# A decoder step with tanh gates, decays queued after attention, sample products among later projections and state updates queued after each FFN block

## The chip, the cores and the metric

The kernel runs on one core of one Trainium2 chip. The metric is the time of one execution in microseconds, as the device counts it; lower is better.

## The reference

One layer of a hybrid decoder, for a prompt of 256 tokens and for 8 sequences that each add one token (264 columns in all). All is fp32. Cut to what matters here:

```python
D_MODEL = 2048; SEQ = 256; DEC_BATCH = 8; WINDOW = 128
SSD_HEADS = 32; SSD_HEAD_DIM = 64; D_STATE = 128; D_FF = 5632

def ssd_mixer(z, xbc, dt_raw, ...):
    xbc, conv_new = causal_dwconv(xbc, conv_past, conv_w, conv_b)
    ...
    y, h_last = ssd_scan(xs, dt, a, bm, cm, h0, chunk)     # chunks of 128
    y = y + xs * d_skip
    y = y.reshape(b, t, D_SSD) * jax.nn.silu(z)
    y = rms_norm(y, norm_g)
    return y, conv_new, h_last

def conv_ffn(x, past, g_ffn, w_up, conv_w, conv_b, w_down):
    u, new_past = causal_dwconv(rms_norm(x, g_ffn) @ w_up, past, conv_w, conv_b)
    gate, val = jnp.split(u, 2, axis=-1)
    return (jax.nn.silu(gate) * val) @ w_down, new_past

def _layer(x, ...):
    proj = rms_norm(x, g_mix) @ w_in            # q | k | v | z | x,B,C | dt
    attn = swa_banded(...)                      # or swa_step for the 8 samples
    ssd, new_conv, new_h = ssd_mixer(...)
    x = x + concatenate([attn, ssd]) @ w_out
    x = x + cross_attend(x, mem_k, mem_v, ...)  # 256 memory tokens
    f, new_ffn = conv_ffn(x, ...)
    return x + f, (new_k, new_v, new_conv, new_h, new_ffn)
```

Inside `ssd_scan`, the decay between two tokens of a chunk is `exp(la_l - la_s)` for l >= s. The new states of the 8 samples, `h * exp(dt a) + x dt B`, are an output of 32 heads x 64 x 128 numbers for each sample.

## The kernel before, in words

Features lie on the 128 partitions, and the 264 tokens are the columns. A matrix product in fp32 is made of three products of split numbers, high x high, high x low and low x high (`mm3`, lines 102 to 104). The weights stream: `weights` (L69) starts the load of a unit of 128 x 2048 numbers (1 MB, `wraw`, two buffers) on SyncE's queue; ScalarE casts each half of it to `whi` (L87), and VectorE subtracts to get `wlo` (L88). `whi` and `wlo` have four buffers each, so the casts can be at most four halves ahead of TensorE. One half feeds 24 matmuls of 264 columns. The second operand, the activations, is split in the same way (`split`, L92).

The stages follow each other in the span: the input projection with q, k and dt (to about 100 us), windowed attention for the prompt (`attn_prompt`) and the samples, x, B and C with their convolution (`conv_group`), the scan of the prompt by groups (`ssd_prompt`, with the decays `e`), the gate (`z_pair`, eight pairs of 128 features, from about 345 us), the output projection `w_out` (its attention half first, eight units, `AT`; then the half of the scan, `Y`), cross attention, and the FFN from about 675 us to the end. In the FFN, 44 blocks each take two `w_up` units, are evacuated (`u`, L1074), convolved (`c`, L1089 on ScalarE, L1091 on VectorE), gated with Silu (L1093) and split (`hh`, `hl`); after each group of eight blocks come units of `w_dn`.

The work for the 8 samples goes along: `ssd_sample(g)` loads old states on GpSimd's DMA queue (L691) and makes the products C*h on VectorE (L692, L693); `gate_sample` combines them to `ysam`, gates and splits it into the last columns of `Y`; `new_state(k, q)` loads old states `hn` on SyncE's queue (512 KB for two calls, three buffers), scales them on ScalarE (L1046), adds x dt B on VectorE (L1047) and stores them from GpSimd's queue (L1050). `memory_norm` loads the memory tokens `mraw` into a pool that opens after the mixer's pool is closed, so these loads come after what the mixer's pool still does, `gate_sample` among it. `accy` sums the squares of the gated y for its norm; `ry` is the reciprocal root of it.

The order of instructions on each engine is made by the scheduler from a simulated timeline; an engine then runs its instructions in that order, and waits at the head of its queue. `tc.high_priority()` lets weight casts go first, and `tc.issue_after(x)` puts what it encloses behind instruction x in the order. Queues that matter: ScalarE, VectorE, GpSimd (also issuing DMAs), SyncE (issuing DMAs).

Of the kernel before, what the change touches and what calls it, by code (L numbers as in the profile page):

```python
# [7 lines left out]
F32 = mybir.dt.float32  # L8
F32R = mybir.dt.float32r
AF = mybir.ActivationFunctionType  # L10
ALU = mybir.AluOpType
# [3 lines left out]
D = 2048  # L15
# [32 lines left out]
def hybrid_decoder_step_kernel(ctx: ExitStack, tc: tile.TileContext, I, O):  # L48
# [166 lines left out]
    def sumsq(acc, x, first, w=T):  # L215
        if first:
            S.activation(out=acc, in_=x, func=AF.Square)
        else:
            sq = small.tile([128, T], F32, tag="sq", name="sq")
            S.activation(out=sq[:, :w], in_=x, func=AF.Square)  # L220
            P.tensor_tensor(out=acc, in0=acc, in1=sq[:, :w], op=ALU.add)
# [23 lines left out]
    gssd = pc("g_ssd", 0, KB)  # L245
# [185 lines left out]
    def attn_prompt(j, rq, nrq):  # L431
        pp = j // 4
        for c in range(2):
# [34 lines left out]
            S.copy(out=attn[:, j, c * 128:c * 128 + 128], in_=o[:, 0:128])  # L468

    pq = psum("s")  # L470
# [145 lines left out]
    def ssd_prompt(g):  # L616
        hs = slice(8 * g, 8 * g + 8)
        hp = mp.tile([128, 512], F32, tag="hp", name="hp", bufs=1)
        for c in range(2):
# [6 lines left out]
            for hh in range(2):  # L626
# [4 lines left out]
                for j in range(4):  # L631
                    S.activation(out=e[:, j, :], in_=e[:, j, :], func=AF.Relu, scale=-1.0, bias=la[:, c * 32 + h0 + j:c * 32 + h0 + j + 1])
                S.activation(out=e, in_=e, func=AF.Exp, scale=-1.0)
# [74 lines left out]
    def z_pair(i):  # L708
# [9 lines left out]
        for m in range(2):  # L718
            k = 2 * i + m
            z = zs[m]  # L720
            S.activation(out=z, in_=z, func=AF.Silu)
            y = xs[k // 4][:, k % 4, :TP]
            V.tensor_tensor(out=y, in0=z, in1=y, op=ALU.mult)
            sumsq(accy[:, :TP], y, k == 0, TP)
            split(Y[k // 8][0][:, k % 8, :TP], Y[k // 8][1][:, k % 8, :TP], y, gssd[:, k:k + 1])

    def gate_sample():
# [7 lines left out]
        S.activation(out=zsam, in_=zsam, func=AF.Silu)  # L735
        V.tensor_tensor(out=ysam, in0=ysam, in1=zsam, op=ALU.mult)
        V.tensor_tensor(out=t, in0=ysam, in1=ysam, op=ALU.mult)
# [20 lines left out]
    ssd_sample(1)  # L758
# [3 lines left out]
    ssd_sample(2)  # L762
    ssd_prompt(3)
    for i in range(2, 8):
        z_pair(i)
        if i == 2:
            ssd_sample(3)
        if i in (3, 5, 7):
            res_load()
# [23 lines left out]
    for i in range(8):  # L793
# [5 lines left out]
        if i == 0:  # L799
            gate_sample()  # L800
    ry = total(accy, D, "ry")
# [258 lines left out]

    groups = [list(range(8 * g, min(8 * g + 8, FB))) for g in range(6)]
    w_up, w_dn = I["w_up"], I["w_dn"]

    def up(g):
        H = (T3(apool, 8, F32R, "A", f"hh{g}", 4), T3(apool, 8, F32R, "A", f"hl{g}", 4))
        n = len(groups[g])
        for ii, i in enumerate(groups[g]):
            us = []

            def ev(m, pm, i=i):  # L1070
# [3 lines left out]
                V.tensor_tensor(out=u[:, 2:], in0=pm, in1=r2, op=ALU.mult)  # L1074
# [5 lines left out]
            if 4 <= i < 36:  # L1080
                new_state(i // 2 - 2, i % 2)
            cs = []
            for m in range(2):
# [5 lines left out]
                S.activation(out=c, in_=u[:, 0:TP], func=AF.Identity, scale=w[0], bias=pc("fb", bi))  # L1089
                for t in (1, 2):  # L1090
                    V.scalar_tensor_tensor(out=c, in0=u[:, t:t + TP], scalar=w[t], in1=c, op0=ALU.mult, op1=ALU.add)  # L1091
                cs.append(c)
            S.activation(out=cs[0], in_=cs[0], func=AF.Silu)  # L1093
# [187 lines left out]
```

## Time and profile before

| | us |
|---|---|
| three runs | 1460.23, 1462.5, 1462.5 (median 1462.5) |
| profiled execution | 1458.88 |
| its span, first to last instruction | 1457.1 |
| granted TensorE clock, mean | 0.991 |
| busy: TensorE / VectorE / ScalarE / GpSimd | 1422.7 / 1062.6 / 790.7 / 176.3 |
| DMA | 304.65 MB, mean 209 GB/s |

A row of a timeline has a start, a length, the engine, the line, the operation, out<-in and the count; the bracket at its end tells how long the engine was idle before it and what ended that. A row of groups has the busy time, the mean of one in ns and the idle time before. A row of stretches has start and end, and for each engine the busy time and the number of instructions.

### The profile page before, as it was taken

How to read it: one execution, taken by the hardware profiler on the slowest of the kernel's cores; microseconds unless marked ns; L12 is line 12 of the kernel's file. 1: busy time of each engine (PE TensorE's matmuls, PEld its weight loads, DVE VectorE, ACT ScalarE, POOL GpSimd, SP SyncE). 2: the span in 40 equal slices, each digit the busy share in tenths (PEclk: the TensorE clock that was granted, in tenths of full speed). 3: DMA queues.
4: the chain of work that ended last, by engine and by line, in shares of the span. 5: the costliest groups of instructions: out<-in, count | busy, mean ns of one | idle time of the engine just before them, and what ended most of it. 6: DMA issues, size and time to landing. Idle time of an engine off the chain costs nothing.

```text
span 1457.1 us, 28707 instructions
## 1 busy us (share of the span) xinstructions
PE 1422.7 (98%) x11481; PEld 1394.7 (96%) x11481; DVE 1062.6 (73%) x2033; ACT 790.7 (54%) x1308; POOL 176.3 (12%) x345
## 2 busy tenths in 40 slices
PE   9999999998999999989899999999999999999999
PEld 8998899998899999979899999999999999999999
DVE  6839869998867667779898666667566756665664
ACT  6647745568646456558786453445345434543442
POOL 0000001123214113116112010001000000000000
PEclk9999999999999999999999999999999999999999
DMA  7754346766675555966898555555555455555554
GB/s 257 281 171 145 118 167 212 251 235 225 232 266 184 190 179 204 344 249 251 320 336 291 193 177 176 184 190 175 177 186 188 174 179 188 183 174 180 191 190 148
DMA packets 59366, 304.65 MB, mean 209 GB/s; under 512 B 8864, under 2 KB 13920, under 8 KB 29664
## 3 DMA queue, kind: packets, MB, share of 16 engines
q1 hardware_dynamic: 53728, 283.94, 55.7%
q0 software_dynamic: 5504, 18.88, 3.6%
q8 instruction: 90, 1.47, 0.4%
q14 instruction: 44, 0.36, 0.1%
HBM read 287.06 MB, written 16.28 MB: 208 GB/s over the span
## 4 chain that ended last, share of the span: by engine, by line
PE 80%; DMA 7%; DVE 6%; ACT 4%; issue 2%; POOL 1%; SPq 0%; ACTq 0%; DVEq 0%; POOLq 0%
PE mm L102 17%; PE mm L103 17%; PE mm L104 17%; PE t L102 8%; PE t L104 8%; PE t L103 8%; DVE wlo L88 2%; DMA wraw<-in_w_up_dram 2%; ACT whi L87 1%; DMA wraw<-in_w_out_dram 1%; DMA hn<-in_h_dram 1%; DVE hn L1047 1%; DMA wraw<-in_w_in_dram 1%; PE s L437 1%; POOL qq L871 1%
## 5 line engine op out<-in xcount | busy, mean ns | idle before, releaser
L87 ACT CAST whi<-wraw 128x1024 fp32r<-128x1024 f32 x448 | 464.9, 1049 | 531.2 <-PE mm L103 297.2
L88 DVE TENSOR_TENSOR wlo<-wraw,whi 128x1024 fp32r<-128x1024 f32 x448 | 552.2, 1237 | 260.8 <-ACT whi L87 257.2
L104 PE MATMUL t<-x2h,wlo 128*128 128x264 f32 x704 | 198.5, 285 | 4.2 <-DVE wlo L88 4.2
L102 PE MATMUL t<-x2h,whi 128*128 128x264 f32 x704 | 200.2, 285 | 1.5 <-ACT whi L87 1.5
L102 PE MATMUL mm<-x2h,whi 128*128 128x264 f32 x704 | 199.4, 284 | 0.6 <-DVE res L1015 0.6
L103 PE MATMUL t<-x2l,whi 128*128 128x264 f32 x704 | 199.7, 284 | 0.0
L104 PE MATMUL mm<-x2h,wlo 128*128 128x264 f32 x704 | 197.4, 284 | 2.3 <-DVE wlo L88 2.3
L103 PE MATMUL mm<-x2l,whi 128*128 128x264 f32 x704 | 199.2, 284 | 0.0
L103 PE MATMUL mm<-hl,whi 128*128 128x264 f32 x704 | 198.8, 283 | 0.0
L104 PE MATMUL mm<-hh,wlo 128*128 128x264 f32 x704 | 198.6, 283 | 0.0
L102 PE MATMUL mm<-hh,whi 128*128 128x264 f32 x704 | 196.9, 284 | 0.0
L102 PE MATMUL mm<-xh,whi 128*128 128x264 f32 x608 | 177.2, 293 | 0.0
L103 PE MATMUL mm<-xl,whi 128*128 128x264 f32 x608 | 176.2, 291 | 0.0
L104 PE MATMUL mm<-xh,wlo 128*128 128x264 f32 x608 | 175.4, 293 | 0.5 <-DVE wlo L88 0.5
L104 PEld LDWEIGHTS t<-x2h,wlo 128*128 128x128 f32 x704 | 132.0, 189 | 5.1 <-DVE wlo L88 5.1
L102 PEld LDWEIGHTS t<-x2h,whi 128*128 128x128 f32 x704 | 133.2, 189 | 1.7 <-ACT whi L87 1.7
L104 PEld LDWEIGHTS mm<-x2h,wlo 128*128 128x128 f32 x704 | 131.1, 188 | 3.2 <-DVE wlo L88 3.2
L102 PEld LDWEIGHTS mm<-x2h,whi 128*128 128x128 f32 x704 | 132.4, 188 | 1.0 <-issue 0.8
L103 PEld LDWEIGHTS t<-x2l,whi 128*128 128x128 f32 x704 | 133.2, 189 | 0.0
L103 PEld LDWEIGHTS mm<-x2l,whi 128*128 128x128 f32 x704 | 132.5, 188 | 0.0
L103 PEld LDWEIGHTS mm<-hl,whi 128*128 128x128 f32 x704 | 132.4, 188 | 0.0
L104 PEld LDWEIGHTS mm<-hh,wlo 128*128 128x128 f32 x704 | 132.2, 188 | 0.0
(418 smaller groups left out, 3075.1 us busy)
## 6 DMA issues: line engine op xcount, KB each, us to landing
wraw<-in_w_up_dram SPq DMA_DIRECT2D x88, 1024.0 KB, 4.9
wraw<-in_w_in_dram SPq DMA_DIRECT2D x51, 1024.0 KB, 5.1
wraw<-in_w_dn_dram SPq DMA_DIRECT2D x44, 1024.0 KB, 4.9
wraw<-in_w_out_dram SPq DMA_DIRECT2D x24, 1024.0 KB, 4.9
h<-in_h_dram POOLq DMA_DIRECT2D x32, 256.0 KB, 4.4
hn<-in_h_dram SPq DMA_DIRECT2D x16, 512.0 KB, 7.5
out_state_s_dram<-hn POOLq DMA_DIRECT2D x16, 512.0 KB, 6.5
pb<-dram_p SPq DMA_DIRECT2D x4, 1028.0 KB, 10.3
```

The lines of the kernel that those rows point to most:

```text
L87: S.copy(out=hi, in_=x)
L88: V.tensor_tensor(out=lo, in0=x, in1=hi.bitcast(F32), op=ALU.subtract)
L102: PE.matmul(out, wh, xh, start=start, stop=False)
L103: PE.matmul(out, wh, xl, start=False, stop=False)
L104: PE.matmul(out, wl, xh, start=False, stop=stop)
L437: PE.matmul(s3, qT[:, j, c * 128:c * 128 + 128], kbd[:, pp, :, 0:nk], start=True, stop=True)
L871: P.tensor_copy(out=qq[:, :, m], in_=sqs[m][:, TP:T])
L1047: V.scalar_tensor_tensor(out=h[:, b, :], in0=bbs[g][:, b, :], scalar=xds[:, k, b:b + 1], in1=h[:, b, :], op0=ALU.mult, op1=ALU.add)
```

## The change

It has four parts.

1. The gate Silu(z) * y becomes (1 + tanh(z/2)) * z * y, one tanh on ScalarE into a new tile `th`, and one more VectorE instruction; the factor 2 is taken up by halving the norm's gain `gssd` and by dividing the sum of squares by 4D. The same holds for the samples in `gate_sample`. The 15 adds of `accy` go from GpSimd to VectorE.
2. The ScalarE part of the decays `e` (four Relu, one Exp each) is issued only after the last copy of the prompt's attention output.
3. `ssd_sample(1)`, `(2)` and `(3)` move to later places among the z pairs and into `w_out`, `gate_sample` from the first to the fifth of the eight attention units of `w_out`.
4. `new_state` of a FFN block moves behind that block's own evacuation and its own ScalarE convolution.

```diff
-    def sumsq(acc, x, first, w=T):
+    def sumsq(acc, x, first, w=T, on=P):
...
-            P.tensor_tensor(out=acc, in0=acc, in1=sq[:, :w], op=ALU.add)
+            on.tensor_tensor(out=acc, in0=acc, in1=sq[:, :w], op=ALU.add)
...
-    gssd = pc("g_ssd", 0, KB)
+    gssd = cpool.tile([128, KB], F32, name="gssd")
+    V.tensor_scalar(out=gssd, in0=pc("g_ssd", 0, KB), scalar1=0.5, scalar2=None, op0=ALU.mult)
...
-            S.copy(out=attn[:, j, c * 128:c * 128 + 128], in_=o[:, 0:128])
+            marks["attn"] = S.copy(out=attn[:, j, c * 128:c * 128 + 128], in_=o[:, 0:128])
...
-                for j in range(4):
-                    S.activation(out=e[:, j, :], ..., func=AF.Relu, ...)
-                S.activation(out=e, in_=e, func=AF.Exp, scale=-1.0)
+                with tc.issue_after(marks["attn"].ins):
+                    for j in range(4):
+                        S.activation(out=e[:, j, :], ..., func=AF.Relu, ...)
+                    S.activation(out=e, in_=e, func=AF.Exp, scale=-1.0)
...
             z = zs[m]
-            S.activation(out=z, in_=z, func=AF.Silu)
             y = xs[k // 4][:, k % 4, :TP]
+            th = small.tile([128, T], F32, tag="raw", name="th")[:, :TP]
+            S.activation(out=th, in_=z, func=AF.Tanh, scale=0.5)
             V.tensor_tensor(out=y, in0=z, in1=y, op=ALU.mult)
-            sumsq(accy[:, :TP], y, k == 0, TP)
+            V.scalar_tensor_tensor(out=y, in0=th, scalar=1.0, in1=y, op0=ALU.add, op1=ALU.mult)
+            sumsq(accy[:, :TP], y, k == 0, TP, V)
...
-        S.activation(out=zsam, in_=zsam, func=AF.Silu)
         V.tensor_tensor(out=ysam, in0=ysam, in1=zsam, op=ALU.mult)
+        S.activation(out=zsam, in_=zsam, func=AF.Tanh, scale=0.5)
+        V.scalar_tensor_tensor(out=ysam, in0=zsam, scalar=1.0, in1=ysam, op0=ALU.add, op1=ALU.mult)
...
-    ssd_sample(1)
     z_pair(0)
     ssd_prompt(2)
     z_pair(1)
-    ssd_sample(2)
+    ssd_sample(1)
     ssd_prompt(3)
     for i in range(2, 8):
         z_pair(i)
-        if i == 2:
-            ssd_sample(3)
+        if i == 5:
+            ssd_sample(2)
...
         proj([w_out[i]], [AT], ev, tag="t" if i % 2 else "mm")
         if i == 0:
+            ssd_sample(3)
+        if i == 4:
             gate_sample()
-    ry = total(accy, D, "ry")
+    ry = total(accy, 4 * D, "ry")
...
-                V.tensor_tensor(out=u[:, 2:], in0=pm, in1=r2, op=ALU.mult)
+                ffn["ev"] = V.tensor_tensor(out=u[:, 2:], in0=pm, in1=r2, op=ALU.mult)
...
-            if 4 <= i < 36:
-                new_state(i // 2 - 2, i % 2)
...
-                S.activation(out=c, in_=u[:, 0:TP], func=AF.Identity, ...)
+                ffn["c"] = S.activation(out=c, in_=u[:, 0:TP], func=AF.Identity, ...)
...
+            if 4 <= i < 36:
+                with tc.issue_after(ffn["ev"].ins), tc.issue_after(ffn["c"].ins):
+                    new_state(i // 2 - 2, i % 2)
```

ScalarE's order in the input projection, before; `e` are decays, `sq` the squares of the query heads, `whi` the weight casts:

```order
L87 CAST whi_968<-wraw_966 128x1024
L87 CAST whi_972<-wraw_966 128x1024
L632 ACTIVATE e_2751<-e_2751,la_551 128x128 x4
L87 CAST whi_1026<-wraw_1024 128x1024
L632 ACTIVATE e_2759<-e_2759,la_551 128x128 x4
L633 ACTIVATE e_2751<-e_2751 128x512
L632 ACTIVATE e_2795<-e_2795,la_551 128x128 x4
L476 ACTIVATE sq_956<-attn_359 128x256
L87 CAST whi_1030<-wraw_1024 128x1024
L633 ACTIVATE e_2759<-e_2759 128x512
L476 ACTIVATE sq_960<-attn_359 128x256
L633 ACTIVATE e_2795<-e_2795 128x512
```

The same place after the change, and then, on the same engine, the last copy of attention with what follows it:

```order
L87 CAST whi_970<-wraw_968 128x1024
L87 CAST whi_974<-wraw_968 128x1024
L87 CAST whi_1028<-wraw_1026 128x1024
L87 CAST whi_1032<-wraw_1026 128x1024
L479 ACTIVATE sq_958<-attn_361 128x256
L479 ACTIVATE sq_962<-attn_361 128x256
```

```order
L470 COPY attn_361<-t_1533 128x128
L636 ACTIVATE e_2753<-e_2753,la_553 128x128 x4
L636 ACTIVATE e_2761<-e_2761,la_553 128x128 x4
L636 ACTIVATE e_2797<-e_2797,la_553 128x128 x4
L87 CAST whi_2537<-wraw_2535 128x1024
L637 ACTIVATE e_2753<-e_2753 128x512
```

The decays have left the input projection and stand directly behind attention's last copy. ScalarE's order at the first z pairs, before (`u0` to `u2` hold z, L632 and L633 are decays):

```order
L721 ACT_TABLE_LOAD
L721 ACTIVATE u0_559<-u0_559 128x256
L87 CAST whi_4454<-wraw_4452 128x1024
L632 ACTIVATE e_3992<-e_3992,la_551 128x128 x4
L87 CAST whi_4458<-wraw_4452 128x1024
L633 ACT_TABLE_LOAD
L633 ACTIVATE e_3992<-e_3992 128x512
L632 ACTIVATE e_4028<-e_4028,la_551 128x128 x4
L721 ACT_TABLE_LOAD
L721 ACTIVATE u1_561<-u1_561 128x256
```

And after (L727 is the tanh, L636 and L637 the decays):

```order
L727 ACTIVATE th_3909<-u2_565 128x256
L636 ACTIVATE e_3966<-e_3966,la_553 128x128 x4
L637 ACTIVATE e_3966<-e_3966 128x512
L87 CAST whi_4400<-wraw_4398 128x1024
L636 ACTIVATE e_4002<-e_4002,la_553 128x128 x4
L87 CAST whi_4404<-wraw_4398 128x1024
L637 ACTIVATE e_4002<-e_4002 128x512
L220 ACTIVATE sq_3904<-xs0_2185 128x256
```

The table loads between gate and decays are no longer there. ScalarE's order at the start of the FFN, before:

```order
L212 ACT_TABLE_LOAD
L212 ACTIVATE r2_8132<-y_8130,eps_314 128x264
L1046 ACTIVATE hn_8828<-hn_8828,dsb_573 128x128 x8
L1046 ACTIVATE hn_9123<-hn_9123,dsb_573 128x128 x8
L1046 ACTIVATE hn_9432<-hn_9432,dsb_573 128x128 x8
L1089 ACTIVATE c_8271<-u_8264,par_71 128x256
L1089 ACTIVATE c_8276<-u_8267,par_71 128x256
L87 CAST whi_8346<-wraw_8344 128x1024
```

And after:

```order
L212 ACT_TABLE_LOAD
L212 ACTIVATE r2_8167<-y_8165,eps_314 128x264
L1096 ACTIVATE c_8306<-u_8299,par_71 128x256
L1096 ACTIVATE c_8311<-u_8302,par_71 128x256
L1103 ACT_TABLE_LOAD
L1103 ACTIVATE c_8306<-c_8306 128x256
L95 CAST hh0_8179<-c_8311 128x256
L87 CAST whi_8381<-wraw_8379 128x1024
```

The 24 state instructions are gone from here; the next weight cast now stands behind the first block's table load, gate and split. SyncE's order in `w_out`, before, with the loads of the memory tokens (`mraw`), of the memory keys (`kt`) and of weights:

```order
L786 DMA mraw_5468<-in_memT_dram 128x1024
L786 DMA mraw_5480<-in_memT_dram 128x1024
L786 DMA mraw_5494<-in_memT_dram 128x1024
L786 DMA mraw_5508<-in_memT_dram 128x1024
L908 DMA kt_7119<-in_mk_dram 128x1024
L908 DMA kt_7131<-in_mk_dram 128x1024
L78 DMA wraw_5274<-in_w_out_dram 128x2048
```

And after, where `wraw_5571` is the first unit of the scan's half of `w_out`:

```order
L792 DMA mraw_5503<-in_memT_dram 128x1024
L792 DMA mraw_5515<-in_memT_dram 128x1024
L792 DMA mraw_5529<-in_memT_dram 128x1024
L78 DMA wraw_5571<-in_w_out_dram 128x2048
L792 DMA mraw_5543<-in_memT_dram 128x1024
L916 DMA kt_7154<-in_mk_dram 128x1024
L916 DMA kt_7166<-in_mk_dram 128x1024
L916 DMA kt_7178<-in_mk_dram 128x1024
L78 DMA wraw_5629<-in_w_out_dram 128x2048
```

The group of loads is split in two and stands three weight units later.

More of the change, by code (lines that the diff above doesn't have):

```diff
@@ L467, in attn_prompt @@
                               start=kb == 0, stop=kb == nb - 1)
-            S.copy(out=attn[:, j, c * 128:c * 128 + 128], in_=o[:, 0:128])
+            marks["attn"] = S.copy(out=attn[:, j, c * 128:c * 128 + 128], in_=o[:, 0:128])
+    marks = {}
     pq = psum("s")
@@ L629, in ssd_prompt @@
                 nc.sync.dma_start(out=e, in_=dram_la[c, h0:h0 + 4, :].partition_broadcast(128))
-                for j in range(4):
-                    S.activation(out=e[:, j, :], in_=e[:, j, :], func=AF.Relu, scale=-1.0, bias=la[:, c * 32 + h0 + j:c * 32 + h0 + j + 1])
-                S.activation(out=e, in_=e, func=AF.Exp, scale=-1.0)
+                with tc.issue_after(marks["attn"].ins):
+                    for j in range(4):
+                        S.activation(out=e[:, j, :], in_=e[:, j, :], func=AF.Relu, scale=-1.0, bias=la[:, c * 32 + h0 + j:c * 32 + h0 + j + 1])
+                    S.activation(out=e, in_=e, func=AF.Exp, scale=-1.0)
                 V.tensor_tensor(out=e, in0=e, in1=cbm.unsqueeze(1).broadcast_to([128, 4, 128]), op=ALU.mult)
@@ L1059, in past @@
         P.tensor_tensor(out=fpc, in0=fpc, in1=pc("fb", 0, 88).unsqueeze(2).broadcast_to([128, 88, 8]), op=ALU.add)
+    ffn = {}
     groups = [list(range(8 * g, min(8 * g + 8, FB))) for g in range(6)]
@@ L1088, in up @@
                 w = [pc("fw", t * 88 + bi) for t in range(3)]
-                S.activation(out=c, in_=u[:, 0:TP], func=AF.Identity, scale=w[0], bias=pc("fb", bi))
+                ffn["c"] = S.activation(out=c, in_=u[:, 0:TP], func=AF.Identity, scale=w[0], bias=pc("fb", bi))
                 for t in (1, 2):
```

## The prediction

> **What bounds the kernel now.** I read the busy table of the page first, then the total of each wait of TensorE, then the busy time of each engine in stretches of 25 or 125 us (columns: sum, PE, PEld, DVE, ACT, POOL, granted PE clock, DMA share, GB/s), and last the timelines around the gaps.
>
> ```profile
> span 1457.1 us, 28707 instructions
> PE 1422.7 (98%) x11481; PEld 1394.7 (96%) x11481; DVE 1062.6 (73%) x2033; ACT 790.7 (54%) x1308; POOL 176.3 (12%) x345
> PE t L102 <- ACT whi L87: 9.5, 4, 4.0
> 50.00:75.00 25.00, 24.70 (x204) 24.20 (x203) 19.01 (x38) 13.05 (x20) 1.82 (x1) 1.00 0.80 267
> 75.00:100.00 25.00, 21.97 (x156) 21.76 (x155) 8.41 (x10) 11.80 (x24) 0.00 (x0) 0.86 0.61 203
> 200.00:225.00 25.00, 25.00 (x199) 25.00 (x198) 20.41 (x49) 9.85 (x15) 3.76 (x7) 0.93 0.46 159
> 225.00:350.00 125.00, 124.04 (x1035) 118.99 (x1034) 124.76 (x240) 77.10 (x136) 24.37 (x34) 1.00 0.72 247
> 350.00:375.00 25.00, 20.99 (x156) 20.30 (x155) 20.23 (x37) 18.02 (x30) 10.46 (x12) 0.93 0.55 193
> 375.00:400.00 25.00, 23.14 (x198) 21.83 (x197) 20.85 (x42) 18.65 (x28) 3.98 (x4) 1.00 0.69 230
> 425.00:450.00 25.00, 22.85 (x173) 22.13 (x172) 15.49 (x18) 12.12 (x19) 8.66 (x8) 0.93 0.74 282
> 675.00:800.00 125.00, 116.93 (x928) 114.81 (x927) 115.39 (x246) 96.64 (x212) 32.28 (x62) 0.99 0.89 325
> 800.00:925.00 125.00, 125.00 (x1034) 125.00 (x1033) 79.86 (x117) 57.06 (x74) 7.06 (x32) 1.00 0.54 185
> ```
>
> TensorE is busy 98% of the span, so only its idle time and its lowered clock can be won. From 800 to 925 us it is never idle: 1034 matmuls in 125 us, 0.121 us apiece. The stretches that fall short are 75 to 100, 350 to 400, 425 to 450 and 675 to 800 us. In each, TensorE waits for a weight half (`whi` cast on ScalarE, as in the wait row above, or `wlo` on VectorE) or for a small square. The ring holds four halves of 24 matmuls; four times 24 times 0.121 makes 11.6 us, the cover that a late cast has. The four parts of the change fall into these four stretches. I cost each from its own stretch.
>
> **Part 1, decays behind the last attention copy (75 to 100 us).**
>
> ```profile
> 83.30 1.28 ACT L632 ACTIVATE e<-e,la 128x128 f32<-128x128 f32 x4 [7.10 <-DMA e<-dram_la]
> ...
> 90.36 0.61 ACT L633 ACTIVATE e<-e 128x512 f32<-128x512 f32 x1
> 88.74 0.92 PE L478 MATMUL s<-cst,sq 128*128 128x2 f32 x4 [3.03 <-ACT sq L476]
> ```
>
> ScalarE stands at the head of its queue until the load of `e` lands at 83.30, with casts and squares queued behind it, and the squares come only between the twelve Relu and three Exp. TensorE idles 3.03 us and then runs at a lowered clock: 0.86 over 25 us is (1 - 0.86) x 25 = 3.5 us. The matmul count agrees: 156 against 204 in the stretch before, 48 missing at 25/204 = 0.1225 us, 5.9 us. The loads of `e` stay where they are on SP; only ScalarE's 15 instructions move, to about 198 us. Their price there is 3 x 1.28 + 3 x 0.61 = 5.7 us of ScalarE time, in a stretch where it is busy 9.85 of 25 us, and behind a ring of 11.6 us, so I cost it at nothing; without that cover it would be 5.7 us. VectorE reads `e` only in the state-space stage after 225 us. Gain between 3.0 (the gap alone) and 6.5 (gap and clock); taken: 5.5, close to the count, less a little for squares that wait for their own matmuls.
>
> **Part 2, the gate (350 to 425 us).**
>
> ```profile
> L721 ACT ACT_TABLE_LOAD x6 | 7.7, 1283 | 0.1
> L633 ACT ACT_TABLE_LOAD x4 | 5.1, 1283 | 0.1
> L660 ACT ACT_TABLE_LOAD x1 | 1.3, 1283 | 0.0
> 356.34 1.99 ACT L87 CAST whi<-wraw 128x1024 fp32r<-128x1024 f32 x2
> 357.42 0.39 PE L102 MATMUL t<-xh,whi 128*128 128x264 f32 x1 [4.01 <-ACT whi L87]
> 387.17 0.39 PE L102 MATMUL t<-xh,whi 128*128 128x264 f32 x1 [1.86 <-ACT whi L87]
> L569 DVE SCALAR_TENSOR_TENSOR c<-u,par,c 128x256 f32<-128x256 f32 x42 | 20.8, 508 | 0.0
> L723 DVE TENSOR_TENSOR xs<-u,xs 128x256 f32<-128x256 f32 x16 | 6.6, 415 | 5.5 <-ACT u L721 5.5
> L692 DVE TENSOR_TENSOR h<-h,cb 128x512 f32<-128x512 f32 x32 | 21.4, 689 | 3.5 <-DMA h<-in_h_dram 2.5 <-DMA cb<-dram_bc 1.1
> L693 DVE TENSOR_REDUCE ych<-h 128x4 f32<-128x512 f32 x32 | 21.3, 675 | 0.0
> L221 POOL TENSOR_TENSOR accy<-accy,sq 128x256 f32<-128x256 f32 x15 | 17.2, 1148 | 47.3 <-ACT sq L220 46.9
> ```
>
> Silu and Exp take turns and each turn loads a table: 6 + 4 + 1 = 11 loads of 1283 ns, 14.1 us of ScalarE. They stand between the casts (one pair starts only at 356.34), and TensorE waits 4.01 us, then 1.86 us. With tanh, the changed order of ScalarE holds no table load here. What can come back: idle 25 - 20.99 = 4.0 and clock 0.07 x 25 = 1.75 in the first stretch, 25 - 23.14 = 1.9 in the second, 7.6 us together.
>
> The price is on VectorE: 16 instructions (th + 1) * y at 508 ns (the same operation and shape, L569) are 8.1 us, and 15 adds that leave GpSimd at 415 ns (L723, same shape) are 6.2 us, 14.4 us in all. Its idle time from 350 to 400 us is 50 - 20.23 - 20.85 = 8.9 us, and the eight pairs of `ssd_sample(3)`, 8 x (0.689 + 0.675) = 10.9 us, leave this stage for the output projection: 8.9 + 10.9 - 14.4 = 5.4 us of room. Ahead of 350 us VectorE has none (124.76 of 125), but the moved `ssd_sample(1)` leaves that stretch for the z pairs, so the room shifts rather than vanishes. `ssd_sample(3)` goes into the stretch after 425 us, where VectorE is busy 15.49 of 25: hidden, at worst 10.9 - 9.5 = 1.4 us late. GpSimd is rid of 17.2 us, and its state loads, which it issues itself, are no longer held behind adds. Bounds: 7.6 if VectorE keeps its room; -5.5 (8.9 - 14.4) if the sample products do not get out of the way. Taken: 5.0, nearer to the upper end because the room is positive and the ring covers single delays; the 2.6 held back is for casts `wlo` behind two more instructions per block. The edits of constants (gssd halved, `total` over 4D) add one VectorE instruction at the start; nothing.
>
> **Part 3, later sample products and gate (425 to 450 us).**
>
> ```profile
> 419.65 1.77 SPq L786 DMA_DIRECT2D mraw<-in_memT_dram  x4
> ...
> 423.17 0.50 SPq L78 DMA_DIRECT2D wraw<-in_w_out_dram  x1
> 435.85 1.99 ACT L87 CAST whi<-wraw 128x1024 fp32r<-128x1024 f32 x2 [8.53 <-DMA wraw<-in_w_out_dram]
> 436.95 0.53 PE L102 MATMUL t<-ath,whi 128*128 128x264 f32 x1 [2.08 <-ACT whi L87]
> ```
>
> The four loads `mraw` (128 x 1024 f32, 0.5 MB each) and two `kt` go out ahead of a weight unit, which lands 435.85 - 423.17 = 12.7 us after its issue; the cover is 11.6 us, and TensorE idles 2.1 us plus 0.07 x 25 = 1.75 us of clock: 3.9 us. `mraw` takes space of the mixer's pool and so waits for the end of `gate_sample`. As that is now called at i == 4, SP issues three `mraw` three units later, then a weight unit, then one `mraw` and three `kt`, then the next. Ahead of the first unit stand 1.5 MB where it was 3 MB; at the 282 GB/s of this stretch 2.5 MB take 8.9 us, under the cover; with the second group, 5.5 MB in 19.5 us against 11.6 + 5.8 = 17.4 us of cover, which can leave 2 us of a gap. Gain between 0 (the gap comes back there) and 3.9; taken: 3.0, since the first group is clearly covered and the 282 GB/s are not the most that is seen (325 over 675 to 800 us).
>
> **Part 4, new states behind the block's own work (675 to 800 us).**
>
> ```profile
> 682.90 7.15 ACT L1046 ACTIVATE hn<-hn,dsb 128x128 f32<-128x128 f32 x24 [1.04 <-DMA hn<-in_h_dram]
> 684.06 1.79 DVE L213 RECIPROCAL r<-r 128x264 f32<-128x264 f32 x1
> 691.63 3.87 ACT L87 CAST whi<-wraw 128x1024 fp32r<-128x1024 f32 x4
> 695.51 1.28 ACT L1093 ACT_TABLE_LOAD   x1
> 696.81 0.42 ACT L1093 ACTIVATE c<-c 128x256 f32<-128x256 f32 x1
> 692.71 0.39 PE L102 MATMUL t<-x2h,whi 128*128 128x264 f32 x1 [1.53 <-ACT whi L87]
> 695.89 0.39 PE L104 MATMUL t<-x2h,wlo 128*128 128x264 f32 x1 [2.44 <-DVE wlo L88]
> L1046 ACT ACTIVATE hn<-hn,dsb 128x128 f32<-128x128 f32 x128 | 39.3, 390 | 7.3 <-DMA hn<-in_h_dram 7.3
> L1047 DVE SCALAR_TENSOR_TENSOR hn<-bb,xds,hn 128x128 f32<-128x128 f32 x128 | 37.5, 353 | 0.0
> SPq L1043 <- DMA out_state_s_dram<-hn: 33.8, 9, 8.5
> ```
>
> All 128 + 128 state instructions run within ten blocks, 24 of them ahead of the first casts of the stage. Against the dense rate 1034 - 928 = 106 matmuls are missing, 106 x 0.121 = 12.8 us. After, each of 32 blocks issues 4 x 0.390 on ScalarE and 4 x 0.353 on VectorE behind its own evacuation and convolution. A block lasts 4 halves, 11.6 us; without states VectorE is busy 79.86 of 125 us there, 7.4 of 11.6, and ScalarE 5.3: with 1.4 and 1.6 more, both stay under 9. The DMA share is 0.54, so 512 KB in and out per two blocks have room. What stays late is the first block: the changed order of ScalarE puts evacuation, c, c, the table load, Silu and the `hh` cast ahead of the next cast. The reciprocal of r2 ends at 684.06 + 1.79 = 685.85; the first evacuation can follow at once, since what stood ahead of it on VectorE were states. Evacuation, c, a VectorE step, evacuation, c are some 2.5 us (estimate: five steps of 0.42 to 0.6, the lengths that such rows have here): 688.4. The load 1.28 and Silu 0.42 make 690.1, product and `hh` 0.8 (two more such steps) 690.9, and `whi` 3.87/4 = 0.97 more: 691.9. TensorE runs out at 692.71 - 1.53 = 691.2, so 0.7 us are left, and about as much for `wlo`. Bounds: 12.8 less both gaps and the spell at half clock (1.53 + 2.44 + 1.75), 7.1, up to 12.8. Taken: 10.0.
>
> In this part one term depends on the table load. The row shows 1.28 us and the next instruction 1.30 us after its start. The Trainium skill, "ScalarE: Activation LUTs", section "What ACT_TABLE_LOAD costs", gives 1283 ns plus a drain of about 1380 ns, 2.66 us per switch; by it the first cast would come 1.4 us later and the sum would be 1.4 us less. The trace shows the 1283 and no drain.
>
> The lowered clock enters parts 1 to 4 with 1.75 us or more wherever a gap was over 2 us (0.93 in 425 to 450, gap 2.08; 1.00 in 375 to 400, gap 1.86). The Trainium skill, "TensorE: Matmul & The Clock Gate", section "HAM oscillation", has the rule that idle gaps over about 3.4 us lower the clock; by it the spell after the gap of 2.08 us would not belong to it, and would stay: 1.75 us less. The trace does not agree, it has the spell.
>
> **Sum.** 5.5 + 5.0 + 3.0 + 10.0 = 23.5. For new waits of a few tenths in 32 blocks I take off 1.0: 22.5. The profiled execution took 1458.9 us (its span 1457.1 and 1.8 around it): 1436.4. The median of the runs, 1462.5, stands 3.6 above that execution, the lowest 1.3: predicted 1440.
>
> **Rivals.**
> VectorE becomes the bound from 345 to 450 us: its new 14.4 us lie where casts `wlo` also stand, and part 2 gives nothing or costs 5.5. For it: 124.76 of 125 just ahead. Against: the 5.4 us of room. Sum 22.5 - 5 to 22.5 - 10.5: 1445 to 1450.5.
>
> The first FFN blocks keep their loss, because loads, not the state instructions, limit them (DMA share 0.89): part 4 gives its lower bound 7.1 or less and part 3 nothing: 22.5 - 2.9 - 3 = 16.6 at best, about 1446 to 1452. Against: the share 0.89 comes from state loads and stores that the change spreads.
>
> All gaps close: 5.9 + 7.6 + 3.9 + 12.8 = 30.2, 1458.9 - 30.2 + 1.3 = 1430. Against: the table load at 688 and the evacuation chain remain.
>
> Slower: SP stands at a state load until the store that frees its buffer has landed, and weight loads queue behind it. The row says 9 such waits, 33.8 us, the longest 8.5. There are 13 loads that reuse one of three buffers, now spread among weight units. Below the cover of 11.6 us the hold costs nothing; each us above it costs 13. Part 4's 10 and the other 12.5 are gone when it reaches 11.6 + 22.5/13 = 13.3 us at every load. At 14.5 us: 13 x 2.9 = 38, 1440 + 38 = 1478. Against: nothing of that length is in the trace.
>
> The parts do nothing (another wait ends last at each place): 1462. Against: the waits at these four places name the moved instructions.
>
> **Chances.** Forecast (1435 to 1445) 0.60; VectorE bound 0.14; FFN loss stays 0.10; all gaps close (1430 to 1434) 0.09; slower 0.04; nothing 0.03. The range 1430 to 1452 leaves out the last two and some tails. A measurement of this kernel can tell about 0.2% (3 us) from no change: faster 0.93, same 0.03, slower 0.04.
>
> **What would show it.** No wait of `s` for the square at about 88 us, and PE clock near 1.00 from 75 to 100; no table load at the tanh line, and no wait for `whi` near 357 and 387; VectorE under 24 of 25 us from 350 to 425; the weight unit behind `mraw` landing before the ring is empty; over 1010 matmuls in the first 125 us of the FFN, and DMA share there near 0.65. Wrong if VectorE is full through the z pairs and the cast `wlo` is what TensorE waits for, or if SP's waits at the state loads exceed 11.6 us.

## The result

| | before | changed |
|---|---|---|
| runs, us | 1460.23, 1462.5, 1462.5, 1460.25 | 1435.89, 1444.18, 1438.9, 1436.53 |
| median, us | 1461.38 | 1437.72 |
| profiled execution / span, us | 1458.88 / 1457.1 | 1435.89 / 1434.1 |

The ratio of the times is 0.9846, 95% interval 0.9813 to 0.9879. Predicted were 1440 us, within 1430 to 1452. The page after, its stretches (the same columns as before), the two largest waits of TensorE and SyncE's wait at the state loads (PE is TensorE, DVE VectorE, ACT ScalarE, POOL GpSimd, SPq SyncE's queue):

```profile
span 1434.1 us, 28668 instructions
PE 1413.7 (99%) x11481; PEld 1387.9 (97%) x11481; DVE 1071.7 (75%) x2066; ACT 774.9 (54%) x1297; POOL 149.9 (10%) x330
75.00:100.00 25.00, 25.00 (x209) 24.99 (x208) 10.89 (x12) 11.09 (x14) 0.00 (x0) 1.00 0.69 243
225.00:350.00 125.00, 124.44 (x1031) 118.91 (x1030) 122.74 (x240) 73.24 (x135) 20.52 (x30) 1.00 0.70 240
350.00:375.00 25.00, 23.95 (x202) 22.32 (x201) 25.00 (x50) 14.80 (x27) 2.72 (x5) 1.00 0.76 251
375.00:400.00 25.00, 25.00 (x203) 24.47 (x203) 25.00 (x46) 12.39 (x19) 3.04 (x3) 1.00 0.57 202
400.00:425.00 25.00, 22.20 (x183) 21.98 (x182) 19.80 (x44) 13.07 (x22) 0.00 (x0) 1.00 0.64 223
425.00:450.00 25.00, 25.00 (x207) 24.93 (x206) 16.02 (x20) 13.24 (x19) 4.95 (x5) 1.00 0.78 303
675.00:800.00 125.00, 122.01 (x994) 121.49 (x993) 93.16 (x159) 72.57 (x118) 10.12 (x50) 0.99 0.60 208
PE mm L102 <- ACT whi L87: 3.5, 2, 2.8
PE t L102 <- ACT whi L87: 3.0, 1, 3.0
SPq L1051 <- DMA out_state_s_dram<-hn: 19.7, 9, 6.2
```

From 75 to 100 us TensorE is full and at full clock. In the z pairs, 350 to 400 us, it lacks 1.05 us instead of 5.9, though VectorE is now at 25.00 of 25 in both stretches. The gap near 437 us is gone, but 2.8 us are idle between 400 and 425, which was full before. The start of the FFN still lacks 3 us.

The weight matmuls (lines 102 to 104) are 10800 in both traces, so the start of the k-th, counted from 0, can be compared. Changed less before, in us, for one execution each; the last row is the last matmul:

```
k-th matmul   start before   difference   what lies since the row above
   432            67.2         -0.3
   768           120.1         -6.6       decays out of the projection
  2496           398.5        -13.0       z pairs
  2688           422.6         -9.8       a new gap of 2.8 at the start of w_out
  2880           450.5        -14.3       the gap of 437 us is gone
  4416           666.4        -14.6       cross attention
  4608           692.7        -13.6       start of the FFN, its gap still there
  5376           796.7        -22.9       states spread
 10800          1453.6        -23.0
```

### The profile page after: what moved, and what is told of

Same layout as the page of the kernel before. It is cut to its first block, busy times and chain, and to the rows that moved or that the text cites. A ratio compares the mean times of both kernels' runs of the same rounds, so it can differ in the third digit from the quotient of the medians.

```text
span 1434.1 us, 28668 instructions
## 1 busy us (share of the span) xinstructions
PE 1413.7 (99%) x11481; PEld 1387.9 (97%) x11481; DVE 1071.7 (75%) x2066; ACT 774.9 (54%) x1297; POOL 149.9 (10%) x330
## 4 chain that ended last, share of the span: by engine, by line
PE 89%; DVE 4%; DMA 4%; ACT 2%; POOL 1%; issue 1%; SPq 0%; ACTq 0%; DVEq 0%; POOLq 0%
PE mm L103 19%; PE mm L102 19%; PE mm L104 19%; PE t L102 9%; PE t L104 9%; PE t L103 9%; DVE wlo L88 1%; DMA wraw<-in_w_out_dram 1%; DMA vt<-in_mvT_dram 1%; ACT whi L87 1%; PE s L439 1%; DVE kt L924 1%; PE t L208 1%; DVE vt L953 1%; DMA wraw<-in_w_in_dram 1%
## 5 line engine op out<-in xcount | busy, mean ns | idle before, releaser
L102 PEld LDWEIGHTS t<-x2h,whi 128*128 128x128 f32 x704 | 133.1, 189 | 3.2 <-ACT whi L87 3.2
```

The lines of the kernel that those rows point to most:

```text
L102: PE.matmul(out, wh, xh, start=start, stop=False)
```

## The experiments

Every experiment was measured beside the kernel before on the same chip; three chips were used. A difference of two medians under about 3 us I do not read. A trace is one execution, and single executions scatter more: five of the traces below (before, moves alone, states alone and the two twins of the states) have the same order on every engine up to about 680 us, and they reach the 2496th weight matmul between 398.5 and 406.3 us. Four kernels took one part each.

**Decays alone.**

```diff
+            marks["attn"] = S.copy(out=attn[...], in_=o[:, 0:128])
...
-                for j in range(4):
-                    S.activation(out=e[:, j, :], ..., func=AF.Relu, ...)
-                S.activation(out=e, in_=e, func=AF.Exp, scale=-1.0)
+                with tc.issue_after(marks["attn"].ins):
+                    for j in range(4):
+                        S.activation(out=e[:, j, :], ..., func=AF.Relu, ...)
+                    S.activation(out=e, in_=e, func=AF.Exp, scale=-1.0)
```

> Only the decays are queued behind attention's last copy; the rest is as before. Matmul by matmul, the changed kernel gained 6.6 us on the one before between the 540th and the 600th matmul of a projection. Theory (15 ScalarE instructions waiting for a load stood ahead of squares and casts): 6.6 us here too, 1461.4 - 6.6 = 1454.8, and no loss of that at about 200 us, where the instructions now run. Rival (the gain in the full change came because several parts work together, or the 5.7 us of ScalarE time is paid after attention): under 3 us, 1458.5 or more.

Measured: 1447.95 us against 1459.47, ratio 0.9925 (0.9905 to 0.9945): 11.5 us. At its own place it gained what the theory says; the stretches of this run there and at the z pairs:

```profile
75.00:100.00 25.00, 25.00 (x210) 25.00 (x209) 11.61 (x14) 11.24 (x16) 0.00 (x0) 1.00 0.70 240
200.00:225.00 25.00, 25.00 (x199) 25.00 (x198) 23.02 (x47) 9.78 (x13) 4.84 (x9) 0.93 0.68 228
350.00:375.00 25.00, 24.81 (x207) 23.16 (x208) 25.00 (x43) 17.64 (x31) 10.83 (x11) 1.00 0.69 235
375.00:400.00 25.00, 25.00 (x207) 24.35 (x202) 25.00 (x41) 16.87 (x25) 10.39 (x6) 1.00 0.59 199
```

TensorE is full where it lacked 3 us, and still full where the decays went. By the 768th weight matmul the gain is 6.9 us. The rest came far from the edit: 4.2 more by the 2496th and 2.3 in the output projection (0.5 was lost again behind it), where neither gate nor loads were touched. The scheduler had made another order there too. For example, the loads ahead of the sixth unit of `w_out` are one `kt` fewer. The waits of 4.01 us at 357 and of 1.86 at 387 are gone, although this kernel still has Silu and eleven table loads between gate and decays (six, three and two at their lines, where the kernel before has six, four and one).

**New states alone.**

```diff
-            if 4 <= i < 36:
-                new_state(i // 2 - 2, i % 2)
...
+            if 4 <= i < 36:
+                with tc.issue_after(ffn["ev"].ins), tc.issue_after(ffn["c"].ins):
+                    new_state(i // 2 - 2, i % 2)
```

> Only the new states are queued behind each block's evacuation and convolution. Theory (256 state instructions stood ahead of casts): 8.5 us, as the full change gained between the start of the FFN and its fourteenth block: 1453. Rival (loads limit the first blocks; they have less to do in the full change only because something else spread them): under 3 us.

Measured: 1451.41 us, ratio 0.9946 (0.9916 to 0.9975): 8.1 us, as expected by the theory. What carries the gain, instructions or traffic, this run does not tell; two runs below ask it.

**Gate alone** (tanh, halved gain, sum over 4D, adds on VectorE; the samples' gate too).

```diff
...
-            S.activation(out=z, in_=z, func=AF.Silu)
...
+            S.activation(out=th, in_=z, func=AF.Tanh, scale=0.5)
...
+            V.scalar_tensor_tensor(out=y, in0=th, scalar=1.0, in1=y, ...)
+            sumsq(accy[:, :TP], y, k == 0, TP, V)
...
```

> Only the tanh gate with its adds on VectorE; sample products and sample gate stay at their old places. Theory (11 table loads of 1.28 us stood between the casts): the gap of 4.0 us at 357 us and its spell of lower clock go, about 5 to 6 us: 1456. Rival (VectorE is the bound: 14.4 us more on it while ssd_sample(3) is still in this stage): TensorE then waits for wlo between 350 and 425 us, and the time is 1460 or more.

Measured: 1454.23 us, ratio 0.9964 (0.9949 to 0.9979): 5.2 us. The median fits the theory, the place does not. From the 2088th to the 2304th weight matmul the traced execution wins 5.3 us, and by the 2496th they are lost again in a new gap; ScalarE and TensorE there:

```profile
382.50 1.99 ACT L87 CAST whi<-wraw 128x1024 fp32r<-128x1024 f32 x2 [2.99 <-DMA wraw<-in_w_in_dram]
383.59 0.59 PE L102 MATMUL t<-xh,whi 128*128 128x264 f32 x1 [4.47 <-ACT whi L87]
```

The cast waited for a weight unit, not for a table. Another 4.6 us are won between the 2688th and the 2880th, at 437 us, though no sample work was moved. But this execution (1458.34 us) is the slowest of the ten and ends only 0.6 us ahead of the kernel before, so its trace does not show where the 5.2 us of the medians are won.

**Moves alone.**

```diff
-    ssd_sample(1)
     z_pair(0)
     ssd_prompt(2)
     z_pair(1)
-    ssd_sample(2)
+    ssd_sample(1)
...
-        if i == 2:
-            ssd_sample(3)
+        if i == 5:
+            ssd_sample(2)
...
         if i == 0:
+            ssd_sample(3)
+        if i == 4:
             gate_sample()
```

> Only the sample products and the sample gate are moved, with Silu and with the adds on GpSimd. Theory (memory loads were ahead of a weight unit in SyncE's queue when the ring ran empty): the gap of 2.1 us at 437 us and its spell of lower clock go, 3 to 4.5 us: 1457.5. Rival (the moves only bring VectorE the room that the tanh needs, and bring nothing alone): 1460 to 1462.

Measured: 1459.24 us against 1459.47, ratio 1.0001 (0.9986 to 1.0017): no gain, as the rival has it. The gap of 437 us is there:

```profile
438.88 2.00 ACT L87 CAST whi<-wraw 128x1024 fp32r<-128x1024 f32 x2 [7.53 <-DMA wraw<-in_w_out_dram]
439.97 0.39 PE L102 MATMUL t<-ath,whi 128*128 128x264 f32 x1 [3.12 <-ACT whi L87]
```

It is 3.12 us long where it was 2.08, but that is scatter. The two traces hold the same operations on the same tiles (named without buffer numbers) in the same order on all five engines: the scheduler has put the moved work back to its old places. So this run shows that the edit does nothing by itself; it does not test what later sample products would do, and the rival's reason, room for the tanh, is not shown.

SyncE's order goes with something else. W is a weight unit of `w_out`, m a load of memory tokens, k one of memory keys, in the order of the queue:

```
before          WWWWWmmmmkkWkWWWWWWWWW
moves alone     WWWWWmmmmkkWkWWWWWWWWW
decays alone    WWWWWmmmmkWkkWWWWWWWWW
gate alone      WWWWWWWWmmmmkkkWWWWWWW
all but moves   WWWWWWWWmmmmWkkkWWWWWW
all but gate    WWWWWmmmmkWkkWWWWWWWWW
changed         WWWWWWWWmmmWmkkkWWWWWW
adds on GpSimd  WWWWWWWmmmmkkkWWWWWWWW
```

The loads stand three units later (two with the adds on GpSimd, a run below) in each kernel with the tanh gate, and at their old place in each without it. The moves change nothing in it by themselves. Why the scheduler puts them there with the tanh gate is open, and no run moves these loads alone.

**All but the moves.** The diff is the change without the lines of the run above.

> The full change without its third part: sample products and sample gate stay at their old places. In the changed kernel TensorE waits 2.8 us at 404 us for a weight unit of w_out that was not there before. Theory A (VectorE is full there because of the tanh's and the adds' instructions): with ssd_sample(3) back in the z stage VectorE is fuller still, the gap of 404 us is longer and the gap of 437 us is back: 1437.7 + 4 to 9 = 1442 to 1447. Theory B (the moved sample products make that gap): it is gone, the gap of 437 us is back, about 1438.

Measured: 1437.34 us (four runs within 1.3 us), ratio 0.985 (0.981 to 0.9891). The full change has 0.9846, measured on another chip. Here the moves do change the order, from about 370 us on, but no gain by them is seen in company either. Neither theory is right on all points: the gap at 404 us is there, 0.95 us, and shorter, not longer, and the gap at 437 us is not back.

**Adds on GpSimd.**

```diff
-            sumsq(accy[:, :TP], y, k == 0, TP, V)
+            sumsq(accy[:, :TP], y, k == 0, TP)
```

> The full change with the 15 adds of accy back on GpSimd. Theory (VectorE is full from 350 to 400 us and the late wlo holds back the buffer of a weight unit): VectorE has 15 x 0.41 = 6.2 us less, the unit is asked for earlier, the gap of 2.8 us at 404 us shrinks below 1: 1437.7 - 2 = 1435.5. Rival (an add on GpSimd, 1148 ns, slows the VectorE instructions beside it by about as much as it takes off): no difference, 1437 to 1439, or slower.

Measured: 1440.72 us, ratio 0.9868 (0.9819 to 0.9917), 3.4 us above "all but the moves" on the same chip. The changed kernel did not run on that chip, and its ratio, 0.9846, lies within this interval; so no gain, as the rival has it, and a loss only as far as the moves bring nothing. The expectation started from this chain in the changed kernel:

```profile
394.93 0.33 SPq L78 DMA_DIRECT2D wraw<-in_w_out_dram  x1
393.69 1.21 DVE L88 TENSOR_TENSOR wlo<-wraw,whi 128x1024 fp32r<-128x1024 f32 x1
402.94 2.00 ACT L87 CAST whi<-wraw 128x1024 fp32r<-128x1024 f32 x2 [8.97 <-DMA wraw<-in_w_out_dram]
404.04 0.39 PE L102 MATMUL mm<-ath,whi 128*128 128x264 f32 x1 [2.81 <-ACT whi L87]
```

The weight load goes out as soon as `wlo` has freed its buffer at 394.9, and lands 8.0 us later. With the adds back on GpSimd this gap indeed went (400 to 425 us: 25.00 busy), but others came, and VectorE did not get its 6.2 us. Its groups, of the changed kernel and then of this run:

```profile
L88 DVE TENSOR_TENSOR wlo<-wraw,whi 128x1024 fp32r<-128x1024 f32 x16 | 19.7, 1245 | 0.0
L99 DVE SCALAR_TENSOR_TENSOR yl<-xs,gssd,yh 128x256 fp32r<-128x256 f32 x8 | 3.8, 469 | 0.0
```

```profile
L88 DVE TENSOR_TENSOR wlo<-wraw,whi 128x1024 fp32r<-128x1024 f32 x14 | 18.9, 1367 | 0.0
L99 DVE SCALAR_TENSOR_TENSOR yl<-xs,gssd,yh 128x256 fp32r<-128x256 f32 x10 | 6.2, 623 | 0.0
```

From 350 to 400 us the 14 `wlo` are 122 ns longer each, the 10 `yl` 154 ns: 1.7 + 1.5 = 3.2 us, about the eight adds (3.3 us) that VectorE has there in the changed kernel. So VectorE got no room, as the rival says. But this execution lost no time there: from the 768th to the 2688th weight matmul it took 298.2 us, the changed kernel 299.4. It lost behind that, 243.8 us against 238.9 from the 2688th to the 4416th, where it has its loads one unit earlier and TensorE idles 1.48 us ahead of 458.9. What makes it no faster is thus open.

**All but the gate** (Silu and adds on GpSimd as before).

> The full change with Silu back in the gates, and with the adds of accy on GpSimd as before; decays, moves and new states as changed. Theory (table loads between casts): the gap of 4 us near 357 us is back with its spell of lower clock, 5 to 7 us lost: 1437.7 + 6 = 1443.7. Rival (the gate's gain is only a shift of a wait for late weight units, as in the run with the gate alone, where a gap of 4.5 us came 20 us later): under 2 us lost.

Measured: 1441.13 us against 1436.05 of the changed kernel on the same chip, 5.1 us lost; ratio 0.9886 (0.9853 to 0.9918). The size fits the theory, the place is another: near 357 us TensorE does not wait for `whi`. It does at 329.7, and ScalarE's rows ahead show what for:

```profile
324.01 1.28 ACT L636 ACT_TABLE_LOAD   x1
...
326.47 1.28 ACT L724 ACT_TABLE_LOAD   x1
...
328.61 1.98 ACT L87 CAST whi<-wraw 128x1024 fp32r<-128x1024 f32 x2
329.69 0.39 PE L102 MATMUL t<-xh,whi 128*128 128x264 f32 x1 [2.34 <-ACT whi L87]
```

Two table loads, 2.56 us, stand ahead of a pair of casts, and TensorE waits 2.34; with the decays alone the same two loads stand there and it waits 1.92. So table loads can stop it, where the order lets several stand ahead of one pair of casts: four before 357 us in the kernel before, two here. They did not cost the 5.1 us, though. This execution is 4.6 us behind the changed one by the 2088th weight matmul; by the 2616th it is 0.2 behind, since it lacks the other's gap at 404; and it is 2 to 6 us behind from the 2880th on, where its loads stand at the old place.

**State traffic alone, and state instructions alone.** Two twins of the kernel before. The first leaves out the 256 instructions and stores the states as they were loaded; the second leaves out 13 of the 16 loads and of the 16 stores, so most of its states are not the right ones.

```diff
# traffic alone
-            S.activation(out=h[:, b, :], in_=h[:, b, :], func=AF.Copy, ...)
-            V.scalar_tensor_tensor(out=h[:, b, :], ...)
+            pass
```

```diff
# instructions alone
-            hns[k] = fp.tile([128, 8, 128], F32, ...)
-            nc.sync.dma_start(out=hns[k], in_=I["h0"][k])
+            if k < 3:
+                hns[k] = fp.tile([128, 8, 128], F32, ...)
+                nc.sync.dma_start(out=hns[k], in_=I["h0"][k])
+            else:
+                hns[k] = hns[k - 3]
...
-        if q:
+        if q and k > 12:
```

> The kernel before, with the loads and stores of the sample states but without the 128 ScalarE and 128 VectorE instructions that compute them; so the states that it stores are the old ones. All 16 loads and 16 stores may now run as early as before or earlier. Theory (instructions ahead of the casts make the loss of the first FFN blocks): 8 us or more gained, 1453 or less, with the DMA share in the first 125 us of the FFN as high as before. Rival (loads and stores limit these blocks): under 3 us gained, TensorE waits for weight units there.

> The kernel before with all 128 + 128 state instructions, but with 3 of the 16 state loads and 3 of the 16 stores; the states computed from the third on are not the right ones, and most are not written. It is the twin of the run with the traffic alone. Theory after that run (the 16 MB of state traffic within 110 us delays the weight loads; instructions matter little): at least 5 us of the loss from 675 to 800 us is gone, 1454 or less. Rival (instructions ahead of casts cost as much by themselves): with no load to wait for they crowd even more, the loss is 12 us or more as before, 1459 or more.

Measured: 1462.98 us, ratio 1.0025 (1.0002 to 1.0048), with the traffic alone, and 1463.56 us, ratio 1.004 (1.0022 to 1.0059), with the instructions alone. Nothing was won by leaving out either. The stretch from 675 to 800 us with the states spread, with traffic alone, and with instructions alone:

```profile
675.00:800.00 125.00, 123.31 (x1001) 122.83 (x1001) 94.60 (x153) 72.82 (x117) 21.51 (x56) 0.99 0.65 226
```

```profile
675.00:800.00 125.00, 116.13 (x899) 113.99 (x898) 81.89 (x116) 59.41 (x87) 35.20 (x67) 0.96 0.85 319
```

```profile
675.00:800.00 125.00, 114.72 (x900) 113.73 (x899) 113.05 (x246) 95.88 (x212) 22.97 (x54) 0.95 0.60 212
```

With traffic alone VectorE and ScalarE have room (81.89 and 59.41 of 125), the DMA share is 0.85, and 899 matmuls run; here casts wait for weight units, 10.8 us from 695 to 800. With instructions alone the DMA share is 0.60, VectorE is full to 750 us (113.05 in all), and 900 matmuls run. The kernel before had 928 with both. The instructions alone run closer together, since they no longer wait for loads: from 684 to 740 us on ScalarE, where they ran from 683 to 781. The traffic alone runs about as before, its loads from 681 to 771 us (674 to 771). So my theory of the first twin (instructions make the loss) and that of the second (traffic makes it) both fell as single causes. Either one, crowded into the first blocks, takes about what both took: from the 4416th to the 5376th weight matmul 133.1 and 133.8 us, the kernel before 130.4, the states spread 121.4. The change spreads both, and no run spreads one of them alone.

**past() late.** `past()` is four GpSimd instructions of 128 x 704 that work out the old columns' share of the FFN's convolution for the samples.

```diff
-            if i == 3:
-                past()
...
+                ffn["fn"] = P.tensor_copy(out=fnew[...], ...)
...
+            if i == 3:
+                with tc.issue_after(ffn["fn"].ins):
+                    past()
```

> The full change with the four GpSimd instructions of past() issued only after the copies of the fourth FFN block. In the changed kernel they run from 664 to 672 us, and two wlo beside them take 5.08 us where two take 2.35 elsewhere; the reciprocal, and with it the first evacuation, comes that much later, and TensorE waits 2.98 us at 679 us. Theory: the chain is 2.3 us earlier, the gap 0.7 us and its spell of lower clock (1.75 us) gone: 4 us, 1433.7. Rival (the pair of wlo is slow because of DMA or ScalarE, not GpSimd): no difference.

Measured: 1433.34 us, ratio 0.982 (0.9777 to 0.9863); the changed kernel had 0.9846 on another chip. So both ran once more on one chip.

> The changed kernel itself, for a comparison on one chip with the version that runs past() late: 1437.7.

> The version with past() late, on the same chip as the changed kernel. Theory: the gap at the start of the FFN and its spell of lower clock are gone, 4 us under the changed kernel: 1433.7. Rival: the 4 us seen between two chips is scatter, under 2 us.

Measured: 1436.05 us (1433.21 to 1439.71) for the changed kernel, 1435.12 (1431.33 to 1436.58) with past() late. The rows of VectorE and GpSimd in the changed kernel's first profile, then VectorE's row and the FFN's first stretch with past() late:

```profile
667.24 2.56 POOL L1066 TENSOR_TENSOR fpc<-fpc,ftmp 128x704 f32<-128x704 f32 x1
665.81 5.08 DVE L88 TENSOR_TENSOR wlo<-wraw,whi 128x1024 fp32r<-128x1024 f32 x2
679.09 0.59 PE L102 MATMUL t<-x2h,whi 128*128 128x264 f32 x1 [2.98 <-ACT whi L87]
```

```profile
670.11 2.35 DVE L88 TENSOR_TENSOR wlo<-wraw,whi 128x1024 fp32r<-128x1024 f32 x2
675.00:800.00 125.00, 125.00 (x1034) 124.89 (x1032) 97.85 (x160) 73.66 (x119) 19.97 (x55) 1.00 0.64 225
```

The mechanism holds: the pair takes 2.35 us again, and the FFN's first 125 us are as full as its later ones (1034). But in cross attention, from 625 to 650 us, the granted clock was 0.73 in this execution and 0.93 in the changed kernel's on that chip; there it lost 3 us, so both reach the 4800th weight matmul at 704.8. At its own place the edit won 2.4 to 4.7 us in the traces (the next table); the 0.9 us of the medians is under what these runs can tell. It is not shown to beat the changed kernel in time.

**All traces, stage by stage.** The time between weight matmuls, in us, for one execution of each kernel. The first column ends behind the projection's decays, the second behind the z pairs and the gap at 404, the third behind cross attention, the fourth in the FFN. From there to the last matmul every trace takes 656.7 to 656.9.

```
                     to 768   768-2688   2688-4416   4416-5376
before                120.1      302.5       243.7       130.4
moves alone           118.0      306.6       245.1       128.4
state traffic alone   119.4      311.1       243.7       133.1
state instr. alone    118.9      306.4       242.4       133.8
states alone          120.1      305.4       242.5       121.4
gate alone            120.8      303.9       240.6       130.9
decays alone          113.2      298.4       242.7       129.6
all but gate          113.9      299.2       244.7       119.9
all but moves         114.7      299.3       238.6       123.4
adds on GpSimd        115.3      298.2       243.8       121.4
changed               113.5      299.4       238.9       122.1
changed, again        115.2      299.0       240.5       119.8
past() late           114.4      302.7       239.2       117.4
past() late, again    113.4      300.2       243.6       117.4
```

Each column splits by one thing. The first splits by the decays, 113.2 to 115.3 us with the edit and 118.0 to 120.8 without. So does the second, 298.2 to 300.2 us against 302.5 to 311.1, but for one execution of 302.7 with a gap of 3.43 us near 407; and not by the gate: the two kernels with late decays and Silu (298.4 and 299.2) are as fast there as those with tanh. The third splits by the place of the loads in SyncE's queue: 238.6 to 240.6 us with eight weight units ahead of them (243.6 where the clock was 0.73), 242.4 to 245.1 with five or seven. The fourth splits by the states.

## Why the prediction was right, point by point

The sum was 22.5 us, and the execution gained 23.0. Parts alone, by medians: 11.5 + 8.1 + 5.2 + 0.2 = 25.0 against 23.7 together. By the steps:

- **Part 1, 5.5 taken.** Right in mechanism and place: 6.6 us by the 768th matmul in the full change, 6.9 alone; the kernels with late decays get there 5.3 us earlier on average. The cover after attention held, at no cost. That the edit alone would gain another 5 us elsewhere, most of it at the z pairs, the prediction had no step for.
- **Part 2, 5.0 taken.** The gap went, but the step "What can come back" failed: it lays the waits at 357 and 387 to the table loads, and the decays alone remove them with as many table loads in place. Table loads ahead of a pair of casts can stop TensorE (2.34 us in the run without the gate), but from the 768th to the 2688th matmul the run without the gate takes 299.2 us and the changed kernel 299.4. What the gate is worth by medians, 5.1 us, shows behind that, in part 3's place. The price step failed too. I wrote that VectorE has 5.4 us of room, and it is at 25.00 of 25 in both stretches. The sample products did not leave: I took 10.9 us off, but they were 6.7 us from 350 to 400, and 9.9 after (rows below). The rival "VectorE becomes the bound" came true there for 2.8 us: a late `wlo` holds the buffer, the weight unit is asked for late, TensorE stops at 404. Of the sign of being wrong, VectorE full and TensorE waiting for `wlo`, the first half came, and the second through the weight unit.
- **Part 3, 3.0 taken.** The gap of 437 us went, 4.5 us, but the step that failed is the cause: "As that is now called at i == 4, SP issues three `mraw` three units later". The moves alone leave every engine's order as it was, and all but the moves has the loads late. In the runs they go late with the gate. That the later loads make the gain fits all 14 traces, but no run moves them alone, so it is argued. The gap itself is not in every execution of the old order: in the five traces it was 2.08, 3.12 and 1.23 us, and under 0.8 in the other two.
- **Part 4, 10.0 taken.** 8.3 us from the 4416th to the 5376th. The term was mis-sized by the first block: 0.7 us of gap forecast, 2.98 measured (1.51 in the second trace of the changed kernel), and 994 matmuls ran in the first 125 us where over 1010 was the sign. The chain from the reciprocal's end to the end of the first cast was 6.4 us where I had 6.05, but the reciprocal ended 3.5 us ahead of TensorE running out, not 5.3 as before; two `wlo` beside past() took 5.08 us. The mechanism as written, "state instructions ... ahead of the first casts", is half of it, since the traffic alone takes as much. I had put the traffic only as a rival, with the price of the loss staying.
- **The clock in all four parts.** A lowered spell does not follow every gap over 2 us: behind the gap of 2.81 us at 404 the granted clock stayed at 1.00 (the last section says more).
- The slower rival, SyncE held at a state load, stayed harmless: the longest such wait is 6.2 us where it was 8.5, and the cover is 11.6.

The sample products of part 2 from 350 to 400 us, before and then changed:

```profile
L693 DVE TENSOR_REDUCE ych<-h 128x4 f32<-128x512 f32 x5 | 3.4, 674 | 0.0
L692 DVE TENSOR_TENSOR h<-h,cb 128x512 f32<-128x512 f32 x5 | 3.3, 680 | 0.0
```

```profile
L697 DVE TENSOR_REDUCE ych<-h 128x4 f32<-128x512 f32 x8 | 5.4, 670 | 0.0
L696 DVE TENSOR_TENSOR h<-h,cb 128x512 f32<-128x512 f32 x6 | 4.5, 757 | 0.0
```

Parts 1 and 4 came as forecast in place, about 1 us over and 2 us under. That the places of parts 2 and 3 gained 8.0 us together, the 5.0 + 3.0 taken, is luck: the first gained by the decays, the second by an order of loads that comes with the gate.

The chain at the FFN's first block, with its table load, in ScalarE's rows after the change:

```profile
675.48 1.28 ACT L1103 ACT_TABLE_LOAD   x1
676.77 0.42 ACT L1103 ACTIVATE c<-c 128x256 f32<-128x256 f32 x1
677.99 3.89 ACT L87 CAST whi<-wraw 128x1024 fp32r<-128x1024 f32 x4
```

The Silu starts 1.29 us after the start of the load. The Trainium skill, "ScalarE: Activation LUTs", section "What ACT_TABLE_LOAD costs", has about 1380 ns of drain on top; this trace again shows none.

## What to carry to other kernels

Where a scheduler orders the queues, an edit also changes the order in places that it does not name: compare the order of each queue, and run each part alone and the whole without it, before a gain is put down to a part. An edit that leaves every queue as it was has tested nothing. Cutting all traces at the same matmuls shows which stage goes with which edit. When two things come together, as instructions and the transfers that feed them, taking one away can leave the loss whole: what is left, crowded into the same place, can cost as much. A sum that comes out right is no proof of its terms.

## What was unexpected of the hardware

GpSimd's fp32 work makes VectorE's slower beside it: a pair of `wlo` took 5.08 us beside past() and 2.35 without; adds of 128 x 256 moved to GpSimd lengthened `yl` from 469 to 623 ns. And the clock is lowered by different amounts in the same place: from 625 to 650 us, with idle gaps of at most 1.7 us, it was 0.93 in one execution of the kernel with past() late and 0.73 in the next, on another chip, and from the 2688th to the 4416th weight matmul the second took 4.5 us more.

How long a gap is does not settle whether the clock falls; where it lies does. In each of the 14 traces the clock falls to half for 3.41 us or a whole multiple of it (but for a last spell that the trace's end cuts off), and the starts of all these spells in a trace are whole multiples of 3.41 us apart, as if on a fixed grid. The gap of 2.08 us ahead of 436.95 in the kernel before lies inside one step of that grid (433.6 to 437.0), and the clock falls at 437.0. The gap of 2.81 us ahead of 404.04 in the changed kernel is cut by the grid at 402.4 into 1.2 and 1.6 us, and the clock stays. Behind the first 14 us and away from the stretches of small matmuls (near 210 us and from 570 to 660), a full-speed step with over 1.75 us idle was always followed by a lowered one, 28 times; of the steps with less idle time, four were, with 1.34 to 1.69 us.
